# When the second tile's key searches run in a block of attention, experts and a recurrent mixer

## The chip, the cores and the metric

The kernel runs on one core of a Trainium2 chip. The metric is the device time of one execution in microseconds, as the median of several runs. The profile is one further execution, taken by the hardware profiler; its times count from the first instruction of the program.

## The reference, cut to what matters

Two blocks work on 256 tokens of 1,024 channels. The first block ends in a layer of experts: for every token and each of 8 heads, two sets of 128 keys are scored, the 16 best of each set are found, their 50 useful sums are ranked, and the 16 best pairs name 16 of 16,384 experts.

```python
sc = jnp.einsum('bshcd,hckd->bshck', q, sub_keys)
sv, si = lax.top_k(sc, PEER_TOPK)
cand_s = (sv[..., 0, :, None] + sv[..., 1, None, :]).reshape(B, S, PEER_HEADS, n_cand)
...
top_s, top_j = lax.top_k(cand_s, PEER_TOPK)
eidx = jnp.take_along_axis(cand_i, top_j, axis=-1)
...
act = jax.nn.gelu(jnp.einsum('tnd,td->tn', u, xt)) * gt
return jnp.einsum('tn,tnd->td', act, v)
```

The second block has a mixer that is a recurrence (a scan in two directions) with a state that first runs over 256 tokens of a context, which does not depend on the first block, and then over the 256 tokens themselves, which do. A gated, convolved feed-forward layer ends it.

## The kernel before, in words

The 256 tokens are two tiles of 128, t = 0 and 1. The experts' stage goes over units (t, h): the 8 heads of tile 0, then the 8 heads of tile 1. A unit gathers 16 rows of 8 KB for each of 128 tokens (L868, an indirect DMA issued by GpSimd, 1 MB each, into 9 buffers G), takes 16 dot products on VectorE (L873), makes the weights in groups of 4, and adds the second halves of the rows to the result, half on TensorE (L898, with a diagonal matrix from ScalarE), half on VectorE (L902). A buffer G is free when its addition is done.

What a unit needs before its gathers: `subkeys` makes the scores of one head for both tiles (TensorE, weights from the SP queue; `sc[g][0]` and `sc[g][1]`, 128 x 256); `best` finds the 16 best of each half on VectorE (L477 MAX8, L478 FIND_INDEX8, L480 MATCH_REPLACE8, L481), changing the scores in place; `pairs` forms the 50 sums on GpSimd (L501, 14 instructions); `route` ranks them and makes the expert numbers on VectorE (L513 to L527), `weigh` the gate.

Order. Each engine runs its own queue in order. The order in the queues is written by a scheduler that walks the program with its own estimate of times: of what is ready, what stands earlier in the program goes first. `issue_after(i)` puts what is traced inside it, as far as it is on i's engine, behind i in that engine's queue. For tile 0, heads 1 to 7 are prepared one to two heads ahead (AHEAD). `best(1, g, ...)` for heads 1 to 7 stands right behind the unit of tile 0 in which the head's scores were made (L932, L933). For tile 1, `pairs`, `route` and `weigh` of head g are traced in unit (1, g - 1), with their VectorE and ScalarE work tied to the end of an earlier unit: `unit_end[H + g - LEAD]` with LEAD = 3 (L924, L925). unit_end holds the last L902 of each unit, eight for tile 0 and then those of tile 1.

Behind the experts in the program, and so of lower rank, stands the mixer, which fills the engines' free time: the context (L1272 to L1289: normalization, keys and values, then four scans, two directions by two tiles), tile 0 (`front(0)`: the PLE layer, projections; `scans0`: two scans), tile 1 (`front(1)` and its two scans, which need the experts' result of tile 1), then the output and the feed-forward layer. A scan (`scan_local`, L999) starts with two small matrix products (sigmoids L1014, L1018), makes features, builds T and LT by masks (L1122, called from L1136 and L1142), solves a triangular system in about ten dependent steps, and ends in X (L1178), a transfer matrix (L1217) and the state P (L1246).

On-chip memory. The pools of tiles are two stacks in the bytes of each partition, one growing up from the left, one growing down from the right. A pool opened after another was closed may take its bytes; an instruction that writes such a tile comes behind the last use of the tiles that had the bytes before (`reuse_waits`, L97). In the compiled program of the kernel before, pool pa, right, holds bytes 167,200 to 183,584, in the order of its tags: row_ffn (4,096), qp (2 x 2,048), sk (2 x 1,024), and the scores sc (6 x 1,024, at 177,440 to 183,584). Pool pe lies above it, up to 203,040. Both are closed at L934. The context scans' pool pc, left, opened after that, holds 140,736 to 195,008: e, hat, sg, a, kd, bT, kT, R, KT, kW, nbW, X up to 173,504, then q (5 x 1,024, to 178,624), T (3 x 1,024, to 181,696), LT (2 x 1,024, to 183,744), and above them AkT, qw, dW, P. After pc, tile 0's pools take the same bytes: pq0 from 140,736 and w0 (8 weight buffers) 148,928 to 181,696, then ps0 140,736 to 199,104.

Of the kernel before, what the change touches and what calls it, by code (L numbers as in the profile page):

```python
# [25 lines left out]
F32 = mybir.dt.float32  # L26
# [10 lines left out]
NT = 2  # L37
H = 8
# [54 lines left out]
def block_kernel(ctx: ExitStack, tc: tile.TileContext, I, out):  # L93
    nc = tc.nc

    def pool(name, bufs=1, space=None, stack=ctx, side="left"):
        kw = {"reuse_waits": "tile", "side": side} if space is None else {"space": space}  # L97
        return stack.enter_context(tc.tile_pool(name=name, bufs=bufs, **kw))
# [14 lines left out]
    def bank(tag="mm", bufs=4, shape=(128, 512), name=None):  # L113
        return ps.tile(list(shape), F32, tag=tag, bufs=bufs, name=name or tag)
# [15 lines left out]
    def C(n):  # L130
        o, w = _C[n]
        o -= NMASK if o > MASK0 else 0
        return cst[:, o:o + w]
# [87 lines left out]
    def lin1(X, src, T, o):  # L221

        w = stage(src)
        for kc in range(8):
            times(o, [a[:, kc * 128:(kc + 1) * 128] for a in w], [a[:, kc, :T] for a in X], kc == 0, kc == 7)
# [212 lines left out]
    def subkeys_one(t, sc):  # L438

        for c in range(2):  # L440
            p = bank()
            for kc in range(8):
                nc.tensor.matmul(p[:, :128], wq0[:, c, kc * 128:(kc + 1) * 128], h2T[0][:, kc, t * 128:(t + 1) * 128],
                                 start=kc == 0, stop=kc == 7)
            qp = pe.tile([128, 128], F32, tag="qp0", name="qp0", bufs=2)
            nc.scalar.activation(qp, p[:, :128], AF.Copy)
            p = bank()
            last = nc.tensor.matmul(p[:, :128], qp, sk0[:, c], start=True, stop=True).ins
            end = nc.scalar.activation(sc[:, c * 128:(c + 1) * 128], p[:, :128], AF.Copy).ins
        return last, end  # L450

    def subkeys(h):

        qp = pa.tile([128, 2, 256], F32, tag="qp", name="qp", bufs=2)
        for c in range(2):
            p = bank()
            lin1(h2T, I["w_peer_q"][2 * h + c], 256, p[:, :256])
            nc.scalar.activation(qp[:, c], p[:, :256], AF.Copy)
        sk = pa.tile([128, 2, 128], F32, tag="sk", name="sk", bufs=2)
        nc.sync.dma_start(out=sk, in_=I["sub_keys"][h])  # L460
        sc = {t: pa.tile([128, 256], F32, tag="sc", name="sc", bufs=6) for t in range(NT)}
        for t in range(NT):
            p = bank()
            for c in range(2):
                nc.tensor.matmul(p[:, c * 128:(c + 1) * 128], qp[:, c, t * 128:(t + 1) * 128], sk[:, c],
                                 start=True, stop=True)
            nc.scalar.activation(sc[t], p[:, :256], AF.Copy)
        return sc

    def best(t, h, sc):  # L470

        for c in range(2):
            s = sc[:, c * 128:(c + 1) * 128]
            iu = sm.tile([128, TOPK], U32, tag="iu", name="iu", bufs=2)
            for r in range(2):
                v8 = sv[:, t, h, c, r * 8:(r + 1) * 8]
                nc.vector.max(out=v8, in_=s)  # L477
                nc.vector.max_index(out=iu[:, r * 8:(r + 1) * 8], in_max=v8, in_values=s)  # L478
                if r == 0:
                    nc.vector.match_replace(out=s, in_to_replace=v8, in_values=s, imm_value=GONE)  # L480
            nc.vector.tensor_scalar(si[:, t, h, c], iu, float(128 - 127 * c), None, op0=OP.mult)  # L481
# [11 lines left out]
    def pairs(t, h, eng):  # L493


        cs = pg.tile([128, NCAND], F32, tag="cs", name="cs", bufs=2)
        ci = pg.tile([128, NCAND], F32, tag="ci", name="ci", bufs=2)
        for dst, src in ((cs, sv), (ci, si)):
            a, b = src[:, t, h, 0], src[:, t, h, 1]
            for o, i, m, w in strips:  # L500
                eng.tensor_tensor(dst[:, o:o + m * w].rearrange("p (m w) -> p m w", m=m),  # L501
                                  a[:, i:i + m, None].to_broadcast([128, m, w]),
                                  b[:, None, :w].to_broadcast([128, m, w]), op=OP.add)
        return cs, ci

    def route(t, h, cs, ci, early=0):

        eidx[t, h] = pg.tile([128, TOPK], I32, tag="eidx", name="eidx", bufs=5)
        ts = sm.tile([128, TOPK], F32, tag="ts", name="ts", bufs=2)
        tj = sm.tile([128, TOPK], U32, tag="tj", name="tj", bufs=2)  # L510
        for r in range(2):
            v8 = ts[:, r * 8:(r + 1) * 8]
            nc.vector.max(out=v8, in_=cs)  # L513
            nc.vector.max_index(out=tj[:, r * 8:(r + 1) * 8], in_max=v8, in_values=cs)
            if r == 0:
                nc.vector.match_replace(out=cs, in_to_replace=v8, in_values=cs, imm_value=GONE)
        tjf = sm.tile([128, TOPK], F32, tag="tjf", name="tjf", bufs=2)
        nc.vector.tensor_copy(tjf, tj)
        ef = sm.tile([128, TOPK], F32, tag="ef", name="ef", bufs=2)
        for e0, e1 in ((0, early), (early, TOPK)) if early else ((0, TOPK),):  # L520
            n = e1 - e0
            oh = pg.tile([128, TOPK, NCAND], F32, tag="oh", name="oh")[:, :n]
            nc.vector.tensor_tensor(oh, C("iota")[:, None, :].to_broadcast([128, n, NCAND]),
                                    tjf[:, e0:e1, None].to_broadcast([128, n, NCAND]), op=OP.is_equal)
            nc.vector.tensor_tensor(oh, oh, ci[:, None, :].to_broadcast([128, n, NCAND]), op=OP.mult)
            nc.vector.tensor_reduce(ef[:, e0:e1], oh, op=OP.add, axis=AX.X)
            done = nc.vector.tensor_copy(eidx[t, h][:, e0:e1], ef[:, e0:e1]).ins  # L527
        return ts, done

    def weigh(t, h, ts, _=None):  # L530

        nm = sm.tile([128, 1], F32, tag="nm", name="nm", bufs=2)
        nc.vector.tensor_scalar(nm, ts[:, 0:1], -1.0, rs[t], op0=OP.mult, op1=OP.mult)
        gs = sm.tile([128, 1], F32, tag="gs", name="gs", bufs=2)
        gate[t, h] = pg.tile([128, TOPK], F32, tag="gate", name="gate", bufs=5)
        nc.scalar.activation(gate[t, h], ts, AF.Exp, bias=nm, scale=rs[t], accum_out=gs)
        nc.vector.reciprocal(gs, gs)
        nc.vector.tensor_scalar(gate[t, h], gate[t, h], gs, 0.5, op0=OP.mult, op1=OP.mult)
# [293 lines left out]
    pa = pool("pa", stack=sA, side="right")  # L832
# [5 lines left out]
    def after(*ins):  # L838

        st = ExitStack()  # L840
        for i in ins:
            st.enter_context(tc.issue_after(i))
        return st

    sc = {}
# [61 lines left out]
    AHEAD = {1: (1, 2), 2: (3, 4), 3: (5, 6), 4: (7,)}  # L907
    LEAD = 3
    unit_end = []
    for t in range(NT):  # L910
        if t == 1:
            h2[1] = ph.tile([128, D], F32, tag="h2", name="h2")
            nc.sync.dma_start(out=h2[1], in_=h2d)
        pacc = [bank("ac", 2) for _ in range(2)]
        for h in range(H):
            if t == 0:
                for g in AHEAD.get(h, ()):
                    with after(*ends, first_gather[0]):
                        sc[g] = subkeys(g)
                    best(0, g, sc[g][0])  # L920
                    weigh(0, g, *route(0, g, *pairs(0, g, nc.gpsimd)))
            else:
                for g in range(h + 1 if h else 0, min(h + 2, H)):
                    with tc.issue_after(unit_end[H + g - LEAD]):  # L924
                        weigh(1, g, *route(1, g, *pairs(1, g, nc.gpsimd)))  # L925
            unit_end.append(experts(t, h, pacc))
            if t == 0:
                if h == 0:
                    sc01 = pe.tile([128, 256], F32, tag="sc0", name="sc01")
                    subkeys_one(1, sc01)  # L930
                    best(1, 0, sc01)
                for g in AHEAD.get(h, ()):  # L932
                    best(1, g, sc[g][1])  # L933
    sA.close()  # L934


# [881 lines left out]
```

## Time and profile before

| | us |
|---|---|
| median of 3 runs | 1604.81 |
| lowest and highest of them | 1598.13, 1608.54 |
| the profiled execution's own time | 1591.28 |
| its span, first to last instruction | 1589.5 |
| VectorE busy (DVE) | 1137.5 (72%) |
| TensorE busy (PE) | 1343.0 (84%) |
| GpSimd busy (POOL) | 597.1 (38%) |

The gathers moved 268.45 MB of the 435.12 MB of all DMAs. The busy share is a mean over stages that differ: the attention part to about 280 us, the experts' stage to about 1138, and the rest of the mixer and the feed-forward layer to the end.

### The profile page before, as it was taken

Reading aid. Unit: us, or ns where it says so; the run is one execution under the profiler, and the core shown is the slowest. Engines: PE = TensorE matmul, PEld = TensorE weight load, DVE = VectorE, ACT = ScalarE, POOL = GpSimd, SP = SyncE. Lnnn points to the kernel's source line nnn. Section 1 sums busy time; section 2 is a strip of 40 time slices with the busy share of each in tenths; the row PEclk is TensorE's granted clock in tenths of the full one; section 3 lists DMA queues with packets and bytes.
Section 4 is the critical chain, followed back from the end, with each engine's and each line's share of the span. In section 5 each row is a group of like instructions: output and inputs, shape, how many; then the busy total and the mean of one; then the engine's idle time right before and its main releaser. Section 6 shows DMA issues by size and latency. Waiting matters only on the chain.

```text
span 1589.5 us, 26469 instructions
## 1 busy us (share of the span) xinstructions
PE 1343.0 (84%) x10140; PEld 882.0 (55%) x10140; DVE 1137.5 (72%) x2495; ACT 515.4 (32%) x1290; POOL 597.1 (38%) x599
## 2 busy tenths in 40 slices
PE   7999996988878787798785889878689993699997
PEld 5744554666435454555433345555344692399997
DVE  3991467599968898889757788998526457466676
ACT  3122411233243333333233332332323222244543
POOL 0000000245655566564643464465102102156663
PEclk9999988899988897876897989989899896799999
DMA  9644345898898899896999999989893415446551
GB/s 357 200 144 158 131 146 159 304 343 329 313 386 323 323 397 392 316 390 232 406 418 404 401 393 374 393 329 419 329 361 114 143 61 180 139 133 188 183 187 53
DMA packets 90197, 435.12 MB, mean 274 GB/s; under 512 B 9996, under 2 KB 14620, under 8 KB 57304
## 3 DMA queue, kind: packets, MB, share of 16 engines
q0 software_dynamic: 36864, 268.45, 42.5%
q1 hardware_dynamic: 52488, 163.67, 30.3%
q8 instruction: 80, 1.31, 0.3%
q10 hardware_dynamic: 720, 1.31, 0.2%
q14 instruction: 45, 0.37, 0.1%
HBM read 428.39 MB, written 5.01 MB: 273 GB/s over the span
## 4 chain that ended last, share of the span: by engine, by line
PE 53%; DVE 24%; DMA 10%; issue 6%; ACT 3%; POOL 3%; SPq 0%; DVEq 0%; POOLq 0%; ACTq 0%
PE mm L205 26%; PE ac L898 7%; DVE G L873 7%; DMA G<-in_experts,eidx 5%; PE ac L205 4%; PE mm L952 4%; DVE x L902 4%; POOL G L868 2%; DMA wada<-in_ada 2%; PE tp L205 2%; DMA Ed<-ple_e 2%; DVE acc L401 1%; PE ac L1537 1%; PE ac L406 1%; PE mm L961 1%
## 5 line engine op out<-in xcount | busy, mean ns | idle before, releaser
L868 POOL DMA_INDIRECT G<-in_experts,eidx x256 | 326.7, 1276 | 382.3 <-DVE x L902 203.2
L898 PE MATMUL ac<-G,dg 128*128 128x512 f32 x504 | 284.1, 711 | 66.6 <-ACT dg L896 66.3
L873 DVE SCALAR_TENSOR_TENSOR G<-G,h 128x1024 f32<-128x1024 f32 x256 | 315.3, 1242 | 29.2 <-DMA G<-in_experts,eidx 29.1
L898 PEld LDWEIGHTS ac<-G,dg 128*128 128x128 f32 x504 | 109.5, 229 | 202.2 <-issue 112.3
L194 POOL TENSOR_TENSOR wl<-wr,wh 128x1024 fp32r<-128x1024 f32 x50 | 122.4, 2463 | 132.6 <-ACT wh L192 88.0
L902 DVE SCALAR_TENSOR_TENSOR x<-G,ga,x 128x1024 f32<-128x1024 f32 (+1 forms) x131 | 169.4, 1294 | 1.6
L882 ACT ACTIVATE gd<-dots,gate 128x1 f32<-128x1 f32 x256 | 74.1, 290 | 283.3 <-DVE G L873 276.2
L205 PE MATMUL mm<-wr,big 128*128 128x512 f32 (+1 forms) x352 | 144.4, 565 | 0.0
L401 DVE SCALAR_TENSOR_TENSOR acc<-wada,scv,acc 128x512 f32<-128x512 f32 x112 | 83.5, 775 | 35.7 <-DMA wada<-in_ada 28.5
L205 PEld LDWEIGHTS mm<-wr,big 128*128 128x128 f32 x352 | 63.9, 191 | 71.5 <-issue 69.6
L205 PE MATMUL mm<-bigl,wh 128*128 128x256 f32 x352 | 99.5, 283 | 1.1 <-DVE bigl L339 1.1
L205 PE MATMUL mm<-bigh,wh 128*128 128x256 f32 x352 | 99.3, 283 | 0.8 <-DVE bigh L338 0.8
L205 PE MATMUL mm<-bigh,wl 128*128 128x256 f32 x352 | 99.1, 283 | 0.0
L192 ACT ACTIVATE wh<-wr 128x1024 fp32r<-128x1024 f32 x66 | 69.6, 1059 | 77.5 <-PE mm L205 26.0
L1631 DVE SCALAR_TENSOR_TENSOR facc<-mm,vec,facc 128x189 f32<-128x189 f32 (+2 forms) x176 | 75.4, 430 | 25.1 <-ACT facc L1624 20.8
L792 POOL TENSOR_TENSOR sgt<-sgt 128x512 f32<-128x512 f32 x4 | 5.8, 1469 | 219.7 <-DVE sgt L791 219.7
L205 PEld LDWEIGHTS mm<-bigh,wh 128*128 128x128 f32 x352 | 67.3, 191 | 1.9 <-DVE bigh L338 1.1
L205 PEld LDWEIGHTS mm<-bigl,wh 128*128 128x128 f32 x352 | 67.3, 191 | 1.7 <-DVE bigl L339 1.3
L205 PEld LDWEIGHTS mm<-bigh,wl 128*128 128x128 f32 x352 | 67.2, 191 | 0.4
L205 PE MATMUL mm<-wr,Xh 128*128 128x512 f32 x144 | 65.5, 608 | 0.0
L406 PE MATMUL ac<-cst,acc 128*128 128x1 f32 x128 | 22.4, 297 | 38.8 <-DVE acc L401 38.8
L756 DVE SCALAR_TENSOR_TENSOR yc<-u,vec,yc 128x256 f32<-128x256 f32 x120 | 53.8, 489 | 0.3
(480 smaller groups left out, 2691.1 us busy)
## 6 DMA issues: line engine op xcount, KB each, us to landing
wr<-in_w_in SPq DMA_DIRECT2D x56, 512.0 KB, 9.3
wada<-in_ada SPq DMA_DIRECT2D x48, 512.0 KB, 4.3
wr<-in_ffn_up SPq DMA_DIRECT2D x44, 512.0 KB, 4.5
wr<-in_ffn_down SPq DMA_DIRECT2D x22, 512.0 KB, 4.1
wr<-in_w_att SPq DMA_DIRECT2D x16, 512.0 KB, 3.6
wr<-in_w_gates SPq DMA_DIRECT2D x16, 512.0 KB, 3.6
wr<-in_w_ple_gate SPq DMA_DIRECT2D x16, 512.0 KB, 8.4
wr<-in_w_peer_q SPq DMA_DIRECT2D x14, 512.0 KB, 8.0
```

The source lines that it names most:

```text
L192: nc.scalar.activation(wh[:, :n], w[:, :n], AF.Copy)
L194: e.tensor_tensor(wl[:, :n], w[:, :n], wh[:, :n].bitcast(F32), op=OP.subtract)
L205: nc.tensor.matmul(o, a, b, start=start and i == 0, stop=stop and i == len(l) - 1)
L401: nc.vector.scalar_tensor_tensor(acc[i], wv, c, acc[i], op0=OP.mult, op1=OP.add)
L756: nc.vector.scalar_tensor_tensor(yc[:, j], u[:, j, k:k + 256], cw[:, j, k:k + 1], yc[:, j], op0=OP.mult, op1=OP.add)
L868: ins = nc.gpsimd.indirect_dma_start(out=b, out_offset=None, in_=I["experts"], in_offset=bass.IndirectOffsetOnAxis(ap=eidx[t, h][:, n:n + ...
L873: nc.vector.scalar_tensor_tensor(b[:, :D], b[:, :D], 1.0, h2[t], op0=OP.mult, op1=OP.mult, accum_out=dots[:, n - g:n - g + 1])
L882: nc.scalar.activation(dg_[:, n:n + 1], dots[:, n:n + 1], AF.Copy, scale=gate[t, h][:, g + n:g + n + 1])
L898: nc.tensor.matmul(pacc[q], dg, v[:, q * 512:(q + 1) * 512], start=first and n == to_pe[0], stop=h == H - 1 and n == TOPK - 4)
L902: end = nc.vector.scalar_tensor_tensor(x[:, t, q], v[:, q], c, x[:, t, q], op0=OP.mult, op1=OP.add).ins
L952: nc.tensor.matmul(p[c, b * w:(b + 1) * w], l[c], r[c], start=True, stop=True)
L1631: nc.vector.scalar_tensor_tensor(o, pg_[:, a0 + dy:a1 + dy, b0 + dx:b1 + dx], fw[:, j, k_:k_ + 1], o, op0=OP.mult, op1=OP.add)
```

## The change

The scores of a head are kept in buffers of their own for each tile: 2 for tile 0 and 7 (H - 1) for tile 1, in place of 6 for both. The searches of tile 1's heads 1 to 7 leave their place behind the units of tile 0 and are traced in tile 1's loop, ahead of the `weigh`, `route` and `pairs` of the same head and tied to the end of the same earlier unit as these. Head 0's search stays where it is. No other instruction is changed.

```diff
-        sc = {t: pa.tile([128, 256], F32, tag="sc", name="sc", bufs=6) for t in range(NT)}
+        sc = {t: pa.tile([128, 256], F32, tag=f"sc{t}", name="sc", bufs=(2, H - 1)[t]) for t in range(NT)}
...
             else:
                 for g in range(h + 1 if h else 0, min(h + 2, H)):
                     with tc.issue_after(unit_end[H + g - LEAD]):
+                        if g:
+                            best(1, g, sc[g][1])
                         weigh(1, g, *route(1, g, *pairs(1, g, nc.gpsimd)))
             unit_end.append(experts(t, h, pacc))
             if t == 0:
...
                     best(1, 0, sc01)
-                for g in AHEAD.get(h, ()):
-                    best(1, g, sc[g][1])
```

## Rows read from the trace of the kernel before

**Rows 1.** Stretches: us; busy PE, PEld, DVE, ACT, POOL; PEclk, DMA share, GB/s.

```profile
305.00:432.00 127.00, 112.66 (x440) 77.68 (x439) 123.71 (x490) 38.37 (x127) 60.48 (x142) 0.95 0.86 328
432.00:725.00 293.00, 239.90 (x2323) 140.92 (x2322) 247.62 (x438) 104.84 (x308) 176.50 (x165) 0.85 0.91 358
740.00:1000.00 260.00, 210.31 (x1389) 114.64 (x1390) 198.33 (x374) 88.57 (x257) 115.69 (x130) 0.87 0.94 378
1000.00:1138.00 138.00, 106.12 (x1227) 66.28 (x1226) 124.42 (x230) 42.41 (x138) 70.36 (x52) 0.89 0.92 368
```

**Rows 2.** VectorE groups, 305 to 432 us: count | busy us, mean ns.

```profile
L478 DVE FIND_INDEX8 iu<-sv,sc 128x8 uint32<-128x128 f32 x60 | 16.6, 283 | 0.0
L477 DVE MAX8 sv<-sc 128x8 f32<-128x128 f32 x60 | 14.6, 278 | 0.0
L480 DVE MATCH_REPLACE8 sc<-sv,sc 128x128 f32<-128x128 f32 x30 | 8.1, 273 | 0.0
L481 DVE TENSOR_SCALAR si<-iu 128x16 f32<-128x16 uint32 x30 | 4.8, 175 | 0.0
```

**Rows 3.** Timeline of VectorE, 425 to 437 us: start us, duration us, instruction.

```profile
428.66 0.17 DVE L481 TENSOR_SCALAR si<-iu 128x16 f32<-128x16 uint32 x1
...
435.51 1.27 DVE L988 TENSOR_TENSOR kk<-kc,mm 128x512 f32<-128x512 f32 x2
```

**Rows 4.** Line L873, five units' dots: ns min/median/max, first and last start us.

```profile
L873 DVE SCALAR_TENSOR_TENSOR G<-G,h x16: 1209/1217/1733, 432.2 to 487.4; 128x1024 f32<-128x1024 f32 x16
L873 DVE SCALAR_TENSOR_TENSOR G<-G,h x16: 1214/1220/1254, 491.3 to 531.0; 128x1024 f32<-128x1024 f32 x16
L873 DVE SCALAR_TENSOR_TENSOR G<-G,h x16: 1212/1218/2294, 534.4 to 577.8; 128x1024 f32<-128x1024 f32 x16
L873 DVE SCALAR_TENSOR_TENSOR G<-G,h x16: 1209/1218/1227, 999.7 to 1050.7; 128x1024 f32<-128x1024 f32 x16
L873 DVE SCALAR_TENSOR_TENSOR G<-G,h x16: 1209/1218/1278, 1095.4 to 1133.7; 128x1024 f32<-128x1024 f32 x16
```

**Rows 5.** Timeline of VectorE, 476 to 485 us: first context scan's masks.

```profile
481.27 0.42 DVE L1122 TENSOR_TENSOR T<-mm,cmask 128x256 f32<-128x256 f32 x1
481.61 0.42 DVE L1122 TENSOR_TENSOR LT<-mm,cmask 128x256 f32<-128x256 f32 x1
```

**Rows 6.** Lines of the scans (context, tile 0, tile 1): first and last start us.

```profile
L1018 ACT ACTIVATE a<-mm x4: 592/597/597, 466.7 to 707.5; 128x512 f32<-128x512 f32 x4
L1018 ACT ACTIVATE a<-mm x2: 591/594/597, 925.0 to 1030.2; 128x512 f32<-128x512 f32 x2
L1018 ACT ACTIVATE a<-mm x2: 597/597/597, 1205.4 to 1212.7; 128x512 f32<-128x512 f32 x2
L1246 DVE TENSOR_TENSOR P<-mm,qw x1: 417/417/417, 532.6 to 532.6; 128x256 f32<-128x256 f32 x1
L1289 POOL COPY st<-P x2: 404/670/937, 616.5 to 799.8; 128x256 f32<-128x256 f32 x2
L1217 DVE TENSOR_TENSOR qw<-mm,dW x4: 425/425/425, 1022.4 to 1114.0; 128x256 f32<-128x256 f32 x4
```

**Rows 7.** Timeline of TensorE and VectorE, tile 1's part of the mixer.

```profile
1137.64 1.97 PE L316 MATMUL tp<-ident,x 128*128 128x128 f32 x8 [5.08 <-DVE x L902]
...
1277.32 0.43 DVE L1122 TENSOR_TENSOR T<-mm,cmask 128x256 f32<-128x256 f32 x1
...
1323.99 0.42 DVE L1246 TENSOR_TENSOR P<-mm,qw 128x256 f32<-128x256 f32 x1
```

**Rows 8.** Line L1178 from 770 to 790 us, and the SP queue's timeline there.

```profile
L1178 DVE TENSOR_TENSOR X<-mm,sg x2: 415/420/425, 778.7 to 779.1; 128x256 f32<-128x256 f32 x2
...
779.65 6.75 SPq L188 DMA_DIRECT2D wr<-in_w_ple_gate  x4
```

**Rows 9.** GpSimd: waits in 305 to 432 (total us, times, longest); L501 later.

```profile
POOL cs L501 <- DVE sv L477: 18.8, 8, 6.7
...
L501 POOL TENSOR_TENSOR ci<-si x46: 182/192/1190, 435.9 to 900.1; 128x8 f32<-128x8 f32 x13, 128x4 f32<-128x4 f32 x7, 128x3 f32<-128x3 f32 x7, 128x6 f32<-128x6 f32 x7
```

## Prediction

> **What bounds the kernel now.** I read the table of busy time by stretch first. In the opening of the experts' stage (305 to 432 us) VectorE is busy 123.7 of 127 us while the DMA engines stand at 0.86; later the DMA share is 0.91 to 0.94 and VectorE has 10 to 24% idle [rows 1]. So the opening is bound by VectorE and the rest mostly by the gathers. Then I read VectorE's work in the opening: searches fill much of it [rows 2], the last one issues its last instruction at 428.66, and the first VectorE work of the mixer comes at 435.51, once the searches are over [rows 3]. The mixer of the context and of tile 0 then runs beside the gathers until 1114, as filler, and tile 1's part starts when the experts end, near 1138 [rows 6, 7]. So from 435 to 1138 two chains share the time: the gathers, and the mixer, which is nearly as long. Whatever holds the mixer back comes out behind the experts at almost full price.
>
> **The change, part by part.** *No instruction is added or removed.* Per head a search is two halves of two MAX8, two FIND_INDEX8 (each with a MATCH_VALUE_LOAD), one MATCH_REPLACE8 (with another) and one TENSOR_SCALAR; no DMA belongs to it.
>
> *Opening.* The 15 searches in the window cost 14.6 + 16.6 + 8.1 + 4.8 = 44.1 us [rows 2], 2.9 us each (records overlap, so an upper value; the loads go beside them). Seven leave: 7 x 2.9 = 20 us. VectorE had 3% idle there, so the dots follow: head 2's first dot moves from 432.2 [rows 4] to about 412. Bounds: 8 us (DMA at 0.86 and PE at 0.89 leave only some 14 us of slack, and part of that may not be usable) to 20.
>
> *Scores.* Each head's second-tile scores now live until its search. Pool pa grows by 3 buffers of 1,024 bytes, from 167,200-183,584 to 164,128-183,584. In the order of the tags sc0 gets 174,368-176,416 and the seven sc1 buffers 176,416-183,584. That is the stretch in which the context scan's pool pc has q (from its third buffer), T (178,624-181,696) and both LT (181,696-183,744). These may be written only when the search that last reads the bytes has run. Now all searches are done at 429 and the first T and LT are written at 481.27 and 481.61 [rows 5], so the reuse costs nothing today. After the change the last search is head 7's, issued behind the last accumulation of unit (1,4), the fifth head of tile 1, since H + 7 - LEAD = 12. LT overlaps the buffers of heads 6 and 7, and each scan needs LT before it can solve. So the first context scan stops at its T and LT until then, and behind it the other three scans, tile 0's PLE and projections (their pools pq0 and w0 reuse pc's bytes), and tile 0's two scans. That such reuse is waited for shows in the trace: the last X of the fourth scan is written at 779.1, and the next pool's weight loads are issued from 779.65 on [rows 8].
>
> *When does head 7's search run?* Without the mixer, units take about 43 us: first dot to first dot is 43.1 for head 3 of tile 0 (491.3 to 534.4). The last unit, from 1095.4 to 1133.7 plus one dot pitch, gives 41; the mean of the ten units from 491.3 to 999.7 with the mixer beside them is 50.8 [rows 4]. Head 2 keeps its 59.1 (491.3 - 432.2): 412 + 59 = 471. Ten units x 43 = 430, and 12 for the turn to tile 1 (one h2 buffer, reloaded): 913, and 3 for the search: **916**. Bounds: 471 + 410 = 881 and 999.7 - 8 = 992.
>
> *From 916 on.* Three units remain with the mixer beside them, as before from 999.7 to 1138: 138 us, so the experts end at 1054 instead of 1138. In these the first scan finishes (T at 481.27 to its P at 532.6 was 51 [rows 5, 6]) and the second (starts of a from 466.7 to 707.5 over three periods: 80 each [rows 6]): 131 us. From 1054 the mixer is alone. One scan alone: from its first T to its last output tile 1's later scan took 1277.32 to 1323.99 = 47 us [rows 7], and from a to T the first scan took 466.7 to 481.27 = 15 [rows 5, 6]: 62. Two context scans: 124 - 7 (begun) = 117, to 1171. Tile 0's PLE and projections: tile 1's took 1137.64 to 1205.4 = 68 [rows 6, 7], to 1239 (before, beside the experts, 799.8 to 925.0 = 125 [rows 6]). Two scans of tile 0: 2 x 62 = 124, to 1363 (before 925.0 to 1114 = 189). Then tile 1's part, 1137.64 to the end, 1589.5 - 1137.6 = 452; I take 10 off for PLE work that it can do earlier: 1363 + 442 = **1805 us of span**, 215 more than now.
>
> *Behind the new waits.* On VectorE the search stands before the route of its head, two units ahead of its gathers; it costs nothing where dots wait for landings. On POOL the pairs now wait for the search, and gathers behind them wait too: in the opening such waits were 18.8 us in 8 cases [rows 9]. For seven heads that is 16 us as an upper bound, nothing as a lower one; I take 0, because two units of lead stand between. SP carries the mixer's loads; they move with the mixer. A pair instruction takes 0.19 us as median and up to 1.19 [rows 9]; with 14 a head, seven heads cost POOL 19 to 117 us. By the Trainium skill (SBUF — State Buffer, Who interferes with whom) an operation of GpSimd that reads SBUF is blocked by a VectorE instruction with two SBUF inputs; every dot is one, so by it the pairs stand at the upper value, the search itself (one input) blocks nothing, and the trace's 1.19 agrees.
>
> The sum is against the profiled execution: 1591.28 us for a span of 1589.5. 1805 + 1.8 = 1807, or +215. The median of the runs shown is 1604.81, 13.5 higher, so the forecast on that scale is **1820**. Low end of this case: search at 881, experts' end at 1019, scans at 47 (2 x 47 - 7 = 87), 50 for PLE and projections, 94 for tile 0's scans: 1250 + 442 = 1692, or 1707 on the median's scale. High end: 992, 138, two scans at 80, 125 and 189: 1604 + 452 = 2056; this has the mixer alone as slow as beside the experts, so I cut at 1900, between; I let the lower end go to 1680, for parts of tile 1 that start earlier than I see.
>
> **The rivals.**
> *A. The mixer is held (forecast).* For it: the byte ranges, the mixer's start right after the searches [rows 3], the loads at 779.65 [rows 8]. Against it: no row shows T or LT themselves waiting.
>
> *B. The held bytes don't meet (not slower).* If the seven buffers come to lie elsewhere, or the mixer's tiles need not wait for them, only the moves are left: 20 off the opening, and between none and all of it back later, where VectorE has 10 to 24% idle [rows 1]; I take half. 1604.81 - 10 = 1595; at best 1585, at worst (all 20 back and 16 of POOL's waits) 1621. It decides if T is still first written before 520.
>
> *C. Transfers set the stage.* The DMA share is above VectorE's from 432 to 1000 [rows 1]. If the gathers alone pace the stage and the mixer's delay fits into what is idle, nothing changes: 1605. Against it: the mixer's 680 us don't fit behind 916 in a stage that then ends at 1054. [...]
>
> *D. The pairs block POOL.* The mixer runs on, but each head's pairs hold the gathers behind them: 19 to 117 us less 20 of the opening, near 1650 (30 to 60 exposed). It decides if the gathers' waits on POOL for the search exceed 5 us a head.
>
> **How the numbers follow.** A 0.85, B 0.08, C 0.03, D 0.04. The time is A's, 1820. A's range of 1680 to 1900 holds it some 19 times in 20, 0.81 in all; the other cases lie below it and are, with A's tails, the 2 in 10 left out. About 1% (16 us) is what a measurement can tell from no change. Faster by more: 0.02, of B's best end. Within 1%: the rest of B and C, 0.09. Slower by more: A, D: 0.89.
>
> **What would show it.** Right: L481 at tile 1's searches spread over about 640 to 920, the opening's dots some 15 to 20 us earlier, the first write of T and LT near 916, experts' last dot near 1054 with DMA near 1 and little PE work until 916, then a long stretch up to 1360 with idle VectorE and DMA, and the part from the last transposes of tile 1 to the end unchanged at 450. Wrong: T written near 480 as now; or the mixer alone as slow as before, which would put the end past 1900.

## The result, and the profile after

The changed kernel takes 1783.91 us (median of 4 runs, 1779.51 to 1789.0), the kernel before 1606.51 beside it: a ratio of 1.1112, 95% interval 1.1071 to 1.1153. The forecast was 1820 with a range of 1680 to 1900. The profiled execution after took 1784.36 us for a span of 1782.6, 193.1 more than before; the medians differ by 177.4, since the profiled execution before was some 15 us under its median.

The stretches of [rows 1], after the change (us; busy PE, PEld, DVE, ACT, POOL; PEclk, DMA share, GB/s):

```profile
305.00:432.00 127.00, 108.27 (x425) 75.52 (x424) 113.78 (x368) 38.52 (x128) 70.39 (x141) 0.92 0.84 323
432.00:725.00 293.00, 163.79 (x261) 64.14 (x259) 227.65 (x422) 62.87 (x231) 158.09 (x138) 0.76 0.98 403
740.00:1000.00 260.00, 164.62 (x879) 79.96 (x880) 223.08 (x464) 72.24 (x235) 157.09 (x158) 0.77 0.95 383
1000.00:1138.00 138.00, 119.37 (x1905) 89.34 (x1903) 74.68 (x139) 48.04 (x116) 36.94 (x32) 0.80 0.25 96
...
1070.00:1330.00 260.00, 236.38 (x3331) 169.73 (x3330) 82.00 (x177) 85.07 (x174) 28.50 (x30) 0.86 0.29 98
```

From 432 to 725 TensorE ran 261 matmuls where it had run 2323: the mixer is gone from there, and the DMA engines move 403 GB/s instead of 358. It comes back behind the last search (its first a is at 919.4), and from 1070 to 1330 it is alone: DMA at 0.29, VectorE a third busy.

The put-off searches, VectorE right behind the last of them, and the first masks of the first context scan (against [rows 3, 5]):

```profile
L481 DVE TENSOR_SCALAR si<-iu x14: 160/162/218, 642.0 to 902.7; 128x16 f32<-128x16 uint32 x14
...
902.59 0.24 DVE L481 TENSOR_SCALAR si<-iu 128x16 f32<-128x16 uint32 x2
...
902.89 1.26 DVE L991 TENSOR_REDUCE ss<-sq 128x8 f32<-128x512 f32 x2
...
944.71 0.42 DVE L1122 TENSOR_TENSOR T<-mm,cmask 128x256 f32<-128x256 f32 x1 [1.14 <-PE mm L961]
945.05 0.41 DVE L1122 TENSOR_TENSOR LT<-mm,cmask 128x256 f32<-128x256 f32 x1
```

L991 sums the squares with which the mixer's scans begin; it follows the last instruction of the last search at once. So the hold is there, but it catches the mixer earlier than the prediction had it: not at T and LT, but at the first tiles of the context scans' pool. Nor do these tiles wait for the search to end. The squares (`sq`, in the first buffers of that pool), their input kk, the ScalarE work just ahead of them and the last search's last reading of scores:

```profile
L988 DVE TENSOR_TENSOR kk<-kc,mm x2: 682/686/689, 441.9 to 443.9; 128x512 f32<-128x512 f32 x2
...
899.60 0.29 ACT L882 ACTIVATE gd<-dots,gate 128x1 f32<-128x1 f32 x1 [2.44 <-DVE G L873]
899.80 1.13 ACT L989 ACTIVATE sq<-kk 128x512 f32<-128x512 f32 x2
...
901.25 0.28 DVE L478 FIND_INDEX8 iu<-sv,sc 128x8 uint32<-128x128 f32 x1
```

The input was there at 444.6, and ScalarE had just been idle for 2.44 us, waiting for a dot of the experts: the squares stand behind the unit's L882 in ScalarE's queue, and they start before the search has read its last scores. SyncE's queue and TensorE show the same, a place in the queue (start us, duration us):

```profile
453.74 7.20 SPq L188 DMA_DIRECT2D wr<-in_w_ple_gate  x2
677.04 0.33 SPq L913 DMA_DIRECT2D h<-h2d  x1
677.42 0.81 SPq L1009 DMA_DIRECT2D hat<-in_lora_up  x2
...
908.88 5.82 PE L898 MATMUL ac<-G,dg 128*128 128x512 f32 x8 [7.99 <-ACT dg L896]
914.53 1.02 PE L1012 MATMUL mm<-hat,wT 65*128 65x512 f32 x2
```

The scan's own load waits on SyncE from 461 to 677, behind the load of tile 1's h2, and its first matmul stands behind the experts' until 914.5. Then the dots of three units, and the scans (against [rows 4, 6]):

```profile
L873 DVE SCALAR_TENSOR_TENSOR G<-G,h x16: 1217/1223/1226, 474.7 to 511.8; 128x1024 f32<-128x1024 f32 x16
L873 DVE SCALAR_TENSOR_TENSOR G<-G,h x16: 1205/1218/1226, 853.9 to 892.3; 128x1024 f32<-128x1024 f32 x16
L873 DVE SCALAR_TENSOR_TENSOR G<-G,h x16: 1210/1217/2291, 996.2 to 1041.9; 128x1024 f32<-128x1024 f32 x16
...
L1018 ACT ACTIVATE a<-mm x4: 580/597/598, 919.4 to 1106.4; 128x512 f32<-128x512 f32 x4
L1018 ACT ACTIVATE a<-mm x2: 597/598/598, 1213.9 to 1284.4; 128x512 f32<-128x512 f32 x2
L1289 POOL COPY st<-P x2: 394/396/398, 1062.4 to 1150.3; 128x256 f32<-128x256 f32 x2
L1217 DVE TENSOR_TENSOR qw<-mm,dW x4: 420/425/425, 1275.0 to 1331.5; 128x256 f32<-128x256 f32 x4
```

The experts end 92 us sooner (last dot at 1041.9, before at 1133.7 [rows 4]), tile 0's scans 217.5 later (1331.5, before 1114.0 [rows 6]). After them nothing is new: 1782.6 - 1331.5 = 451 us.

### The profile page after: what moved, and what is told of

Read it like the earlier page. It is cut to its first block, busy times and chain, and to the rows that moved or that the text cites. A ratio compares the mean times of both kernels' runs of the same rounds, so it can differ in the third digit from the quotient of the medians.

```text
span 1782.6 us, 26640 instructions
## 1 busy us (share of the span) xinstructions
PE 1390.7 (78%) x10140; PEld 895.9 (50%) x10140; DVE 1140.5 (64%) x2495; ACT 519.2 (29%) x1285; POOL 613.5 (34%) x599
## 5 line engine op out<-in xcount | busy, mean ns | idle before, releaser
L898 PE MATMUL ac<-G,dg 128*128 128x512 f32 x504 | 327.3, 807 | 241.8 <-ACT dg L896 241.7
L868 POOL DMA_INDIRECT G<-in_experts,eidx x256 | 351.6, 1373 | 334.2 <-DVE x L902 175.6
L873 DVE SCALAR_TENSOR_TENSOR G<-G,h 128x1024 f32<-128x1024 f32 x256 | 312.8, 1231 | 53.2 <-DMA G<-in_experts,eidx 53.2
L898 PEld LDWEIGHTS ac<-G,dg 128*128 128x128 f32 x504 | 126.2, 263 | 429.5 <-ACT dg L896 282.1
L882 ACT ACTIVATE gd<-dots,gate 128x1 f32<-128x1 f32 x256 | 74.1, 290 | 327.9 <-DVE G L873 326.0
L1206 POOL TENSOR_TENSOR dW<-cst,wC 128x256 f32<-128x256 f32 x16 | 11.7, 732 | 138.7 <-DVE qw L1217 135.4
L1023 POOL TENSOR_TENSOR a<-a,rx 128x512 f32<-128x512 f32 x4 | 7.3, 1830 | 137.0 <-DVE kd L1021 73.0
```

The lines of the kernel that those rows point to most:

```text
L868: ins = nc.gpsimd.indirect_dma_start(out=b, out_offset=None, in_=I["experts"], in_offset=bass.IndirectOffsetOnAxis(ap=eidx[t, h][:, n:n + ...
L873: nc.vector.scalar_tensor_tensor(b[:, :D], b[:, :D], 1.0, h2[t], op0=OP.mult, op1=OP.mult, accum_out=dots[:, n - g:n - g + 1])
L882: nc.scalar.activation(dg_[:, n:n + 1], dots[:, n:n + 1], AF.Copy, scale=gate[t, h][:, g + n:g + n + 1])
L898: nc.tensor.matmul(pacc[q], dg, v[:, q * 512:(q + 1) * 512], start=first and n == to_pe[0], stop=h == H - 1 and n == TOPK - 4)
```

## The experiments

Each ran beside the kernel before on the same chip; the ratios are against those runs. **Theories**: H, what the put-off searches keep in memory holds the mixer, by bytes (Hb, the prediction's) or by whole pools (Hp); S, the searches or the pairs in their new place cost the time. The diffs of runs 1 to 5, of run 8 and of runs 11 and 12 are against the kernel before, those of 6, 7, 9 and 10 against the changed kernel. In the diffs `keep` stands for `nc.vector.tensor_copy(sm.tile([128, 1], F32, tag="nm", name="kept", bufs=2), ...)`, a copy of one column that nobody reads.

**1. The buffers alone.**

```diff
-        sc = {t: pa.tile([128, 256], F32, tag="sc", name="sc", bufs=6) for t in range(NT)}
+        sc = {t: pa.tile([128, 256], F32, tag=f"sc{t}", name="sc", bufs=(2, H - 1)[t]) for t in range(NT)}
```

> The kernel before with the changed kernel's nine score buffers (2 for tile 0, 7 for tile 1, so the same 3,072 bytes more) but the searches in their old place. If the time goes because put-off searches hold memory under the mixer, the last search still ends near 429 us, the first context scan starts near 467 and the time is that of the kernel before, 1600 to 1612 us. If the larger pool itself costs (its bytes now reach lower, under earlier tiles), it is above 1620. If the put-off searches' own work or the pairs on GpSimd cost the time, it is also that of before, so this run only clears the buffers.

1591.99 us, ratio 0.9988 (0.9967 to 1.0008), first a at 466.1. The buffers cost nothing.

**2. One late copy, no search moved.** Tied behind unit (1,4), at bytes that no mixer tile uses.

```diff
                         weigh(1, g, *route(1, g, *pairs(1, g, nc.gpsimd)))
+                        if g == H - 1:
+                            keep(sc01[:, 0:1])
```

> The kernel before, all searches early and its six buffers, with one added instruction: VectorE copies one column of head 0's second-tile scores into a small tile that nobody reads, tied behind the fifth unit of tile 1, where the changed kernel has its last search. These scores lie in pool pe at bytes 200,992 to 202,016, above everything that the context scans (up to 195,008) and tile 0's scans (up to 199,104) use. If the mixer waits byte by byte, as the prediction had it, nothing is held: 1600 to 1612 us, first a of the scans near 467. If the mixer's pool waits for the last reader of any tile in the pools under it, the first a moves to about 915 and the time to about that of the changed kernel, 1765 to 1800. If put-off searches or GpSimd's pairs are the cost, none is moved here: 1600 to 1612.

1787.19 us, ratio 1.1219 (1.1194 to 1.1244). Its trace: the searches, the copy and VectorE behind it, the scans' a.

```profile
L481 DVE TENSOR_SCALAR si<-iu x32: 145/158/358, 267.3 to 429.1; 128x16 f32<-128x16 uint32 x32
...
907.97 0.14 DVE L927 COPY kept<-sc 128x1 f32<-128x1 f32 x1
...
908.77 0.67 DVE L993 TENSOR_REDUCE ss<-sq 128x8 f32<-128x512 f32 x1
...
L1020 ACT ACTIVATE a<-mm x4: 592/597/597, 926.1 to 1111.7; 128x512 f32<-128x512 f32 x4
```

All searches are over at 429.1, and an instruction of 0.14 us costs as much as the change (193 us, the change 177). S falls as the main cause. Hb falls too: the copied column lies at 200,992 to 202,016, above all that the context scans and tile 0's scans use (up to 199,104). The mixer comes behind the last reader in the pools beneath it, whatever its bytes.

**3. The same copy from another pool.** `keep(sv[:, 1, 0, 0, 0:1])`: the best values, in the experts' pool, above the mixer's.

> The kernel before with the same added copy, tied behind the same fifth unit of tile 1, but of a column of the best values, whose pool no pool of the mixer lies over until the experts are over. It is the control for the copy of the scores' column that came out at 1787 us. If it is the pool under the mixer that holds it: 1590 to 1605, as before, first a near 467. If an added VectorE instruction tied so late disturbs the order by itself: toward 1787.

1607.37 us, ratio 1.0009 (0.9987 to 1.0032), with the copy at 1013.6.

```profile
L1020 ACT ACTIVATE a<-mm x6: 587/597/597, 467.8 to 1045.0; 128x512 f32<-128x512 f32 x6
```

So neither the copy nor its tie delays anything; the pool that is read does. Whether one pool holds, or the two that are closed together (pa and pe), no run tells apart.

**4 and 5. The copy of 2, earlier.** Behind unit (0,4) or (0,7): the hold alone, in two more sizes.

```diff
                     best(1, 0, sc01)
+                if h == 4:
+                    with tc.issue_after(unit_end[h]):
+                        keep(sc01[:, 0:1])
```

> The kernel before, every search early, with the same copy of one column of head 0's second-tile scores as in the run that came out at 1787 us, but tied behind the fifth unit of tile 0. No search is moved, no buffer added, and no ring of small tiles is stretched, so it is the hold alone. The units without the mixer should take 40 us, the fifth unit ends near 558, the first a comes near 578, 111 us after that of the kernel before. The full hold cost 193 us for 459 us of delay, 0.42 us per us: 47 us more here, a ratio of 1.029 (1.02 to 1.04). If the mixer waits byte by byte, or if the copy is harmless so early: 1.00.

1653.33 us, ratio 1.0332 (1.0274 to 1.0391).

> The same with the copy tied behind the last unit of tile 0, which should end near 682 us; first a near 700, a delay of 233 us, at 0.42 us per us 98 us more: a ratio of 1.061 (1.045 to 1.075). If the price of the hold is not in proportion to its length (little at first, then steep, since the mixer fits beside the experts as long as they last), it is nearer 1.03.

1697.43 us, ratio 1.0604 (1.0542 to 1.0667). The scans' a and the scan's loads in the first, the a in the second:

```profile
L1021 ACT ACTIVATE a<-mm x5: 591/597/597, 578.3 to 1039.2; 128x512 f32<-128x512 f32 x5
L1012 SPq DMA_DIRECT2D hat<-in_lora_up x4: 308/332/366, 448.3 to 632.2; - x4
```

```profile
L1021 ACT ACTIVATE a<-mm x5: 585/597/597, 696.9 to 1124.9; 128x512 f32<-128x512 f32 x5
```

In the first the load went out at 448.3, as before, and a still came at 578.3: SyncE's queue is not the hold. Nor is it a wait for the reader. `hat` is a tile of the scans' pool, and this load fills it 113 us before the copy runs; the squares in the pool's first tiles, whose input was there at 437 and 438, start before the copy as well, in run 4 and in run 5:

```profile
560.81 0.29 ACT L882 ACTIVATE gd<-dots,gate 128x1 f32<-128x1 f32 x1 [1.71 <-DVE G L873]
561.01 1.13 ACT L992 ACTIVATE sq<-kk 128x512 f32<-128x512 f32 x2
...
561.89 0.15 DVE L934 COPY kept<-sc 128x1 f32<-128x1 f32 x1
```

```profile
678.45 1.13 ACT L992 ACTIVATE sq<-kk 128x512 f32<-128x512 f32 x2
...
681.29 0.15 DVE L934 COPY kept<-sc 128x1 f32<-128x1 f32 x1
```

So a late reader in these pools moves the mixer's instructions back in the queues, whose order is written before the program runs; when it runs, they stand behind the experts' work and do not wait for the reader. Why the scheduler puts them there, no run shows.

With the first a at 467.8 as the zero (run 3), 110.5 us of delay cost 50.6 us, 229.1 cost 94.7, 458.3 cost 193.1: 0.46, 0.41 and 0.42 us per us. The rows give that slope, as an estimate that takes the mixer's progress beside the experts as even. Held for d, the experts do d/40 units in place of d/50.8, and so end 0.27 d sooner; the mixer loses 1.27 d beside them. What takes 647 us beside them (a at 466.7 to qw at 1114.0, [rows 6]) would take 357 alone: of 647, 122.5 (919.4 to 1041.9) were done, and the other 81% took 289.6. 1.27 x 357/647 - 0.27 = 0.43.

**6 and 7. The searches themselves, tied earlier.** Last one behind unit (0,4), or one behind each unit up to (0,7).

```diff
-                        if g:
-                            best(1, g, sc[g][1])
...
                     best(1, 0, sc01)
+                for g in {1: (1,), 2: (2, 3), 3: (4, 5), 4: (6, 7)}.get(h, ()):
+                    with tc.issue_after(unit_end[h]):
+                        best(1, g, sc[g][1])
```

> The changed kernel, buffers included, with the seven put-off searches tied earlier: one behind unit (0,1), two each behind (0,2), (0,3) and (0,4), so the last ends near 560 us instead of 903. If the hold of the mixer is the cost, the time follows that end: 11 units are left at the 50.8 us that a unit takes beside the mixer, so the experts end near 1114; 559 of the mixer's 679 us beside them are done by then, the other 18% take 0.18 x 355 = 63 us alone (355: in the changed kernel 20% were done beside the last three units and the rest took 285 us), then 451 for the end: 1628 of span, 1610 to 1660. If being put off costs by itself (searches ahead of the route, pairs and gathers behind them), all seven still are: 1700 or more.

1670.64 us, ratio 1.0374 (1.0334 to 1.0414).

> The same with one search behind each unit (0,1) to (0,7), so the last ends near 690 us. By the hold: 8 units at 50.8 = 406, experts' end 1096; 406 of 679 done, 0.4 x 355 = 142 alone, then 451: 1689 of span, 1660 to 1720, about two thirds of the way in time from before to changed. By the searches' own cost: the same as the run before this one, whatever that is.

1699.23 us, ratio 1.0552 (1.0515 to 1.0588). First a at 599.6 and 705.9: 0.49 and 0.39 us per us. The time follows the end of the last search; the equal times that S asks for did not come. My 1628 for the first was too low: the last search ended at 580, not 560, the first a came 20 us behind it, and the experts' last dot at 1142.9, not 1114. These two have a flaw: a search that waits keeps the two small index tiles (`iu`), so the searches behind it in the text wait too (tile 0's head 3 ends at 422, in the change at 354). Runs 4 and 5 are free of that.

**8 and 9. The hold taken away, at the price of a weight slot.** Scores in the experts' pool; the weight ring has 3 slots, and its control changes that alone.

```diff
-    W2R = 4
+    W2R = 3
...
-        sc = {t: pa.tile([128, 256], F32, tag=f"sc{t}", name="sc", bufs=(2, H - 1)[t]) for t in range(NT)}
+        sc = {t: (pa, pg)[t].tile([128, 256], F32, tag=f"sc{t}", name="sc", bufs=(2, H - 1)[t]) for t in range(NT)}
```

> The kernel before with three instead of four buffers in the ring of weight slots that stays over the experts' stage (4,096 bytes less): the control for the run after this one. The ring feeds the opening's query weights and the mixer's projections; one slot fewer lets fewer loads run ahead. I expect 1600 to 1625 us, no more than 1% over the kernel before; no theory of the change says more of it.

1625.79 us, ratio 1.021 (1.0187 to 1.0234).

> The changed kernel with its seven second-tile score buffers in the pool of the experts' stage that no mixer pool overlaps until the experts are over (room from the weight ring's fourth slot, as in the control). All put-off searches stay where the change put them. If memory held under the mixer is the cost, by bytes or by pools, the first a of the scans comes near 430 to 480 again, and the time is that of the control or up to 15 us less: 1590 to 1615. If the searches' place, the pairs on GpSimd behind them or the gathers behind these are the cost, it stays above 1650, toward 1784.

1638.08 us, ratio 1.0285 (1.0267 to 1.0303); first a at 514.6, in the control 511.2. The hold is gone, but the control is 2.1% over the kernel before, where I had expected at most 1%, and the cured kernel is 0.8% (12 us) above even that and over its forecast of 1590 to 1615.

**10. The hold taken away, nothing else.** Heads 1 to 3 in the experts' pool, heads 4 to 7 in a tile of the mixer's outer pool that is free until tile 1's shifts.

```diff
-        sc = {t: pa.tile([128, 256], F32, tag=f"sc{t}", name="sc", bufs=(2, H - 1)[t]) for t in range(NT)}
+        sc = {t: sc4[:, h - 4] if t and h > 3 else (pa, pg)[t].tile([128, 256], F32, tag=f"sc{t}", name="sc", bufs=(2, 3)[t])
+              for t in range(NT)}
...
+    sc4 = pr.tile([128, 4, 256], F32, tag="Xl", name="sc4")
```

> The changed kernel with all four slots in the weight ring and the put-off scores out of the mixer's way: heads 1 to 3 in the experts' pool, heads 4 to 7 in a tile that the mixer's own pool has free until tile 1's shifts. All put-off searches stay where the change put them. By the hold (pools or bytes) the first a is back at 430 to 470. Then two sizes are open: by the prediction's rival B, up to 20 us come off the opening and half may come back, 1585 to 1600; by the run with three slots, where the same cure came out 12 us above its control, the searches only move from the opening to a stretch in which the mixer needs VectorE: 1600 to 1615. Near 1784, or above 1650, would say that the hold is not the cause.

1626.62 us, ratio 1.0115 (1.0079 to 1.0151). 156 of the 177 us are back. Without the hold the change is no gain either: it costs 21 us, and the time is over both sizes that I had left open (1585 to 1615). The scans' a and the loads of the context's weights in this run:

```profile
L1020 ACT ACTIVATE a<-mm x6: 587/594/597, 487.9 to 1084.8; 128x512 f32<-128x512 f32 x6
L188 SPq DMA_DIRECT2D wr<-in_w_in x8: 327/328/328, 392.6 to 438.3; - x8
```

**11. The seven searches left out.**

```diff
-                for g in AHEAD.get(h, ()):
-                    best(1, g, sc[g][1])
...
-                        weigh(1, g, *route(1, g, *pairs(1, g, nc.gpsimd)))
+                        weigh(1, g, *route(1, g, *pairs(1, 0, nc.gpsimd)))
```

> The kernel before without the seven searches of tile 1's heads 1 to 7 at all; these heads' pairs take head 0's best values, so every other instruction stays (the output is another). It bounds what putting them off can win when nothing is held. If the opening's 20 us of VectorE are what the opening waits for, as the prediction took it: 20 off and nothing back, 1575 to 1592. If the opening waits as much for the gathers and weight loads, 1595 to 1610. In the cured run the context scans began 20 us later than before, although VectorE had less to do: if that comes from the order in which the opening's work is queued once the searches are gone, the first a is near 485 here too; if it comes from the put-off searches, near 450.

1607.93 us beside 1592.6, ratio 1.0096 (1.0069 to 1.0123): less work, and slower. So the 20 us of VectorE in the opening are worth nothing in the whole: head 3's first dot comes 12 us sooner (479.2, before 491.3), the experts' last dot 6.5 us later (1140.2, before 1133.7). Nor are the 21 us of run 10 in the main the searches' own time: 1.0115 and 1.0096 have overlapping intervals, which leave room for some 10 us of it. SyncE's loads in the opening of the kernel before, then of this run with a stretch of [rows 1]'s kind and its scans' a:

```profile
366.71 0.33 SPq L460 DMA_DIRECT2D sk<-in_sub_keys  x1
370.17 0.33 SPq L188 DMA_DIRECT2D wr<-in_w_lora  x1
373.62 50.41 SPq L188 DMA_DIRECT2D wr<-in_w_in  x8
...
430.00:470.00 40.00, 32.85 (x72) 13.77 (x70) 28.27 (x50) 15.81 (x39) 24.23 (x29) 0.87 0.99 381
```

```profile
378.26 0.33 SPq L460 DMA_DIRECT2D sk<-in_sub_keys  x1
379.13 0.33 SPq L188 DMA_DIRECT2D wr<-in_w_lora  x1
388.12 47.57 SPq L188 DMA_DIRECT2D wr<-in_w_in  x8
...
430.00:470.00 40.00, 30.79 (x68) 12.96 (x67) 24.82 (x45) 13.88 (x35) 13.42 (x11) 0.92 1.02 410
...
L1016 ACT ACTIVATE a<-mm x6: 591/597/598, 486.8 to 1070.8; 128x512 f32<-128x512 f32 x6
```

With the searches gone from their place, the last heads' key loads, and behind them on the same queue the context's weights, go out 12 and 14.5 us later; the gathers take the DMA engines instead (1.02 of the share, 410 GB/s), and the first a comes 20 us later. At 0.42 us per us that is 8 of the 15 us. It is so in every kernel without the early searches: w_in from 388 to 393 in runs 6, 7, 10, 11 and in the change, 373 to 376 in runs 1 to 5. That the late loads are the cause, and where the other 7 us are, stays open. The pair with three weight slots speaks against them as the whole: in runs 8 and 9 w_in goes out at 411.2 and 413.1 and the first a comes 3.4 us apart, and run 9, with the searches put off, still takes 12 us more.

**12. Three heads put off, without a hold.**

```diff
-        sc = {t: pa.tile([128, 256], F32, tag="sc", name="sc", bufs=6) for t in range(NT)}
+        sc = {t: (pg if t and h > 4 else pa).tile([128, 256], F32, tag="sc1" if t and h > 4 else "sc", name="sc",
+                                             bufs=3 if t and h > 4 else 6) for t in range(NT)}
...
+                        if g > 4:
+                            best(1, g, sc[g][1])
...
-                    best(1, g, sc[g][1])
+                    if g < 5:
+                        best(1, g, sc[g][1])
```

> The kernel before with only heads 5 to 7 put off, ahead of their pairs as in the change, their three score buffers in the experts' pool, out of the mixer's way; heads 1 to 4 are searched early, in the six old buffers. If the 21 us by which the cured run is slower come from the searches' time on VectorE beside the mixer, 3 of 7 of it: near 1615. If they come from the mixer's later start, which here should be smaller: 1598 to 1610. A gain (under 1595) needs the opening to give back 9 us of VectorE and the rest to hide them.

1599.67 us, ratio 1.004 (1.0017 to 1.0062): w_in from 374.2, as before, first a at 478.0. No gain here either. No version here with searches put off beats the kernel before.

## Why the prediction was right, point by point

**The hold** was forecast with its reason and its place, and runs 2 to 5 show it: the kernel before with one late reader and no other change costs 193 us. Wrong in it was how the hold acts. The prediction let the first scan run up to T and LT, which share bytes with the scores and would wait for the search; run 2 holds the mixer by bytes that nobody shares, and in runs 4 and 5 and in the change the writing of the pool's first tiles starts before the last reader is through, so the mixer is held by its place in the queues. The row that I took for reuse by bytes [rows 8] is a load into another pool; it could not tell how the scans are held, and I did not see that. The prediction had T at once behind the search, at 916; it came 42 us behind it (902.7 and 944.7). Other errors took that back.

**The terms of the sum**, forecast and measured:

| term | forecast | measured |
|---|---|---|
| head 2's first dot (432.2 before) | 412 | 429.5 |
| from there to head 3's first dot | 59 | 45.2 |
| a unit without the mixer | 43 | 39.7 to 42.1 |
| last search ends | 916 | 902.8 |
| experts' last dot | 1054 | 1041.9 |
| context scans end | 1171 | 1150.3 |
| tile 0's PLE and projections | 68 | 63.6 (to 1213.9) |
| tile 0's two scans | 124 | 117.6 (to 1331.5) |
| from there to the end | 442 | 451.1 |
| span | 1805 | 1782.6 |

The 22 us too many are the search's 13 and 8 on the context scans; tile 0's two terms (4 and 6 too many) and the end (9 too few) nearly cancel. That the sum came so near is in part luck, for larger errors cancel inside the terms. Of the 13, head 2's first dot came 17 us later than forecast, its unit was 14 us shorter (45 us in run 2 too, where no search is moved, 432.6 to 477.8), the ten units and the turn were 21 us shorter, and the search behind them ended 7 us later and not 3. Of the 8, the third scan began 161 us behind the search's end and not 131 (the hold's 42 us are in this), while the last two took 43 each alone (1063.8 to 1106.4 to 1149.8) and not 62. The 10 us for work of tile 1 done early were not there: the end kept its 451.

**The opening's 20 us** were the mis-sized term. VectorE's busy time fell by 10 (123.7 to 113.8), and head 2's dots came 2.7 us sooner. Its 97% [rows 1] was read as a bound; the stage then found other waits, for instance the gathers' wait for free buffers (26.6 us from 300 to 432, before 18.0). Run 2, with all searches early and the same hold, has head 2's first dot at 432.6 and the span at 1785.1: by the spans the move of seven searches was worth 2.5 us under the hold. By the medians it could be up to 16 (a rise of 193 in run 2, of 177 in the change, not run beside each other), so its size stays open. Run 11 gives its worth without a hold: below nothing.

**Rival B** said near 1595 if nothing is held. Its condition was made in run 10, and it gave 1626.6 beside 1605.7. What B says of a kernel without the hold was sound in that 156 of the 177 us go; its price had the wrong sign.

**Rival C**: the time did not stay at 1605. The Trainium skill (Perfetto Trace Analysis, Identifying the Most-Contended Engine) has the most-contended engine optimized first, and measures DMA by HBM utilization and not by occupancy. Here, in the stretch from 432 to 725, both measures of DMA rose, the share from 0.91 to 0.98 and the rate from 358 to 403 GB/s, while the span grew by 193 us: a fuller bottleneck engine was no measure of the whole.

**Rival D** needed 5 us a head of GpSimd's waits for the search. Its waits from 640 to 905 (total us, times, longest):

```profile
POOL G L868 <- DVE x L902: 36.3, 21, 4.1
POOL G L868 <- DVE eidx L527: 31.0, 5, 7.3
...
POOL G L868 <- DVE sv L477: 3.3, 5, 0.7
POOL G L868 <- DVE si L481: 0.5, 3, 0.2
POOL G L868 <- DVE iu L478: 0.3, 1, 0.3
```

4.1 us for seven heads, 0.6 a head. The two units of lead cover it, as the prediction took it. The pairs' instructions did not stand at the upper value of 117 us either: the 93 recorded from 640 to 905 took 24 us together, though single ones took up to 1.30 us. What they cost the kernel, no run isolates.

## What to carry to other kernels

Before work is put off, ask what it keeps alive until then, and which pool comes to lie over it: here a 0.14 us reader in the wrong pool cost 193 us. Such a hold need not show as a wait: the held instructions started before the reader and were late by their place in the queues. In this kernel the filler beside the bound stage paid 0.4 us for each us that it started late. A busy share of 97% in one stretch does not make the whole follow that engine: seven searches taken out altogether made this kernel 1% slower. A control tells the price of room: the one weight slot given up for the scores cost 2.1% by itself.

## What the runs showed that was not expected

Less work in a stage can end in more time: run 11 has 20 us less on VectorE and takes 15 us more, with the context's weights loaded 14.5 us later; that these late loads are why is not shown. The gathers alone paced a unit at 40 us, at a DMA share of 0.98 and 403 GB/s, and the mixer beside them stretched it to 50.8 at 0.91 and 358 GB/s: so the mixer took some of the gathers' time although the DMA engines were not full.
